# Hybrid decoder step: a head's normalising factors once instead of three times, output weights loaded one lot ahead, and high priority for bank traffic

## The chip, the cores and the metric

The kernel runs on one core of one Trainium2 chip. The metric is the device time of one execution in microseconds (us). Shown are the median and the extremes of several runs, and one more execution that the hardware profiler recorded: its span, and what each engine did in it.

## The reference

One step of a decoder layer with two parallel branches, for 1024 prompt tokens and 32 sample tokens (8 sequences of 4), model width 1024, all in float32:

```python
h, gate = adaln_in(x, c, w_ada, b_ada, g_norm)        # norm, scaled and shifted
(mq, mk, mv, mi, mf, mo, mz, aq, ak, av, az, gm, ga) = split_in(h @ w_in)
y_m, C, n, m = mlstm_branch(mq, mk, mv, mi, mf, mo, mz, C0, n0, m0, b_i, b_f, g_mn)
o = attn_prompt(q, k, v, sinks)                       # or with the cache, for the samples
y_a = o * jax.nn.silu(az)
u = jax.nn.sigmoid(gm) * (y_m @ w_mo) + jax.nn.sigmoid(ga) * (y_a @ w_ao)
x = x + gate * (u @ w_o)                              # then a last norm
...
def mlstm_chunk(carry, inp):                          # 4 heads, chunks of 128 tokens
    ...
    num = jnp.einsum('bhts,bhse->bhte', s, v) + w_inter[..., None] * jnp.einsum('bhtd,bhde->bhte', q, C)
    dot = jnp.sum(s, axis=-1) + w_inter * jnp.einsum('bhtd,bhd->bht', q, n)
    h = num / jnp.maximum(jnp.abs(dot), jnp.exp(-m_hat))[..., None]
    ...
h = h * lax.rsqrt(jnp.mean(h * h, axis=-1, keepdims=True) + NORM_EPS)
```

The division by the larger of |dot| and exp(-m_hat), followed by the root of the mean square, is what the kernel calls a head's factors.

## The kernel before

**Engines.** TensorE (PE) multiplies; ScalarE (ACT) and VectorE (DVE) move results out of its banks and form operands; SyncE (SP) issues most DMAs, ScalarE and GpSimd (POOL) a few.

**Products.** Every wide product of 1024 tokens is made of pairs: two jobs of 128 output columns together, by seven block products (numbers 1 to 7) in place of eight, on sums and differences of blocks. Each block product is 12 matmuls of 128x512, since a float32 operand is split into a high and a low part (`wh`, `wl` for weights, made by an ACT cast and a DVE subtraction) and three of the four combinations are multiplied. `pairs` lists them: four `head_in` pairs (queries, keys and values of the mLSTM heads), eight `gate` pairs (ga and gm, called ga0 to ga7 in the prediction), two `query_gate` and four `head_gate` pairs. `block_products` runs them in the order 5, 6, 2, 7, 1 of the next pair, 3, 4. A product writes to a bank: bx (products 1, 2), bw (6, 3), by (7, 4), bz (5). `filled` copies one finished bank into the next one that goes on from it, and `done` calls the kind's `evac`, which takes a finished block out (for a gate: a sum, a tanh `gt`, a store). `samples` and `samples_end` make the same jobs' sample columns (smp, smpo; a gate's `samples` takes smpo out as `gts`). `load` asks for the next pair's weights, at product 6.

**Side work.** Between a block's matmuls `side.tick()` gives other work its turn. `Side` (line 112) keeps streams of generators: m (heads, two live), a (attention units: scores sc, their transposes pt), x (sums of blocks), s (sample heads: stk, sU, sn, st, sty), g (the last modulation, then `out_weights`). A generator yields a lag and the kinds of banks that its next visit uses; the lag is counted in `side.now`, an estimate of TensorE's time. So these lags say after how much product work each visit comes. A `store` is issued by SP once 8 units have passed. PE's order is fixed by this; the order on ACT, DVE and POOL between the first part and line 2161 is not, there a scheduler picks by priority, which follows program order where nothing else is said. All banks come from four pools of two: g (bx, bw), a (by, bz), b (transposes tk, tv, ty and stk, smp, smpo, the sample heads' sU) and o (the heads' S, U, n and the sample heads' sn, st). SBUF tiles of 2 KB come from one pool (`ht`).

**A head.** `head(h)` (line 1027) goes through eight chunks in three groups of 3, 3 and 2 chunks (p = 0, 1, 2). Per group: `load` brings q, k, v, the decay matrix et and the weights qw; `prep` adds the mask; `stage_e` takes exponentials; `stage_a` transposes k and v (tk, tv) and forms S; `stage_b` makes U and, from it, the running state C of each chunk; `stage_c` makes n, copies it out as ns (into et's buffer) and sums its squares; `stage_c2` calls `factors`, a row of narrow DVE operations on 3 or 2 columns; `stage_c3` scales ns by them; `stage_d` transposes (ty) and stores. The list of visits at its end gives the order and the lags.

**Output weights.** `out_weights` (line 1924) scales the rows of w_out by the gate gb and stores what the last product needs, in six lots: four of one block row, two of two block rows from which also the sums t1 to t4 are formed. It loads a lot, waits 6 units and multiplies, one tile a visit; the sums are formed in place in the loaded tiles. `OUT_WEIGHTS = 6` starts it at product 6 of pair number 6, ga2.

Of the kernel before, what the change touches and what calls it, by code (L numbers as in the profile page):

```python
# [24 lines left out]
NS = NB * NT  # L25
# [147 lines left out]
def body(tc, a):  # L173
    nc = tc.nc
    with ExitStack() as ctx:
# [799 lines left out]
        vs = cp.tile([128, NH, NS], F32, name="vs")  # L975
        gs = cp.tile([128, NH, NS], F32, name="gs")

        def factors(dot, fl_, ssq, shape, name):
            den = sm(shape, name + "den", 2)
            V.scalar_tensor_tensor(den, dot, -1.0, dot, op0=ALU.mult, op1=ALU.max)  # L980
            V.tensor_tensor(den, den, fl_, op=ALU.max)
            V.reciprocal(den, den)
            v = sm(shape, name + "v", 2)
            V.tensor_tensor(v, den, den, op=ALU.mult)
            V.tensor_tensor(v, v, ssq, op=ALU.mult)
            V.tensor_scalar(v, v, 0.5 / 128, 0.5 * EPS, op0=ALU.mult, op1=ALU.add)
            return den, recip_sqrt(v, shape, name + "r")
# [39 lines left out]
        def head(h):  # L1027
# [71 lines left out]
            def stage_c(p):  # L1099
                cs = GROUPS[p]  # L1100
                m, j0 = len(cs), h * 8 + cs[0]
                vn, et, qw, chain, ns = w_[p]
                num = po([128, 3, 129], f"n{h}_{p}")
                for i, c in enumerate(cs):
                    mm(num[:, i], et[:, i], vn[:, i], start=True, stop=(c == 0))
                    if c:
                        mm(num[:, i], qw[:, i], chain[i], start=False, stop=True)
                S.copy(ns[:, :m], num[:, :m])
                ssq = sm([128, 3], "mssq", 2)
                for i in range(m):  # L1110
                    jk = sm([128, 128], "mjk", 2, BF16)
                    S.activation(jk, ns[:, i, 0:128], AF.Square, accum_out=ssq[:, i:i + 1])
                w_[p] = ns, ssq

            def stage_c2(p):
                m, j0 = len(GROUPS[p]), h * 8 + GROUPS[p][0]
                ns, ssq = w_[p]
                w_[p] = ns, factors(ns[:, :m, 128], fl[:, j0:j0 + m], ssq[:, :m], [128, m], f"f{m}")

            def stage_c3(p):  # L1120
                m = len(GROUPS[p])
                ns, (d, r) = w_[p]
                for i in range(m):
                    V.tensor_scalar(ns[:, i, 0:128], ns[:, i, 0:128], d[:, i:i + 1], r[:, i:i + 1], op0=ALU.mult, op1=ALU.mult)
                w_[p] = ns

            def stage_d(p):
                cs = GROUPS[p]
# [7 lines left out]
                S.activation(y, ty[:, :m].rearrange("p c e -> p (c e)"), AF.Copy, scale=gmn[:, h:h + 1])  # L1136
                issue(yhD[h][:, c0:c0 + w], y, eng=nc.gpsimd)

            for visit in ([(load, 0), 9.0, ""], [(prep, 0), 3.0, "ob"], [(stage_e, 0), (stage_a, 0), 7.0, "o"],
                          [(stage_b, 0), (load, 1), 8.0, ""], [(prep, 1), 3.0, "ob"], [(stage_e, 1), (stage_c, 0), (stage_a, 1), 3.0, ""],  # L1140
                          [(stage_c2, 0), 5.0, "o"], [(stage_b, 1), (stage_c3, 0), (load, 2), 4.0, "b"], [(stage_d, 0), 4.0, ""],
                          [(prep, 2), 3.0, "ob"], [(stage_e, 2), (stage_c, 1), (stage_a, 2), 3.0, ""], [(stage_c2, 1), 5.0, "o"],
                          [(stage_b, 2), (stage_c3, 1), 5.0, "b"], [(stage_d, 1), 5.0, "o"], [(stage_c, 2), 3.0, ""], [(stage_c2, 2), 7.0, ""],
                          [(stage_c3, 2), 5.0, "b"], [(stage_d, 2), 0.0, ""]):
                for fn, p in visit[:-2]:
                    fn(p)
                yield visit[-2:]
# [9 lines left out]
        def sample_head(h):  # L1157
# [73 lines left out]
            d, r = factors(ns[:, 128:129], fls[:, h:h + 1], ssq, [NS, 1], "fs")  # L1231
# [255 lines left out]
        def block_products(jobs, hook):  # L1487
            flat = [(0, 1)]
            for n in range(len(jobs)):
                nx = [(n + 1, 1)] if n + 1 < len(jobs) else []  # L1490
                flat += [(n, i) for i in (5, 6, 2, 7)] + nx if n else [(n, 6), (n, 2), (n, 7)] + nx + [(n, 5)]
                flat += [(n, 3), (n, 4)]

            def split_ahead(j):
                if j < len(flat):
                    jobs[flat[j][0]].split(flat[j][1])

            bank = lambda pool, name: pool([128, 512], name)
            jobs[0].load()
            yield  # L1500
            jobs[0].samples()
            split_ahead(0)
            jobs[0].first_sums()
            split_ahead(1)
            yield

            def filled(pool, name, src, n):
                b = bank(pool, name)
                if n == 0:
                    mm(b, wh[:, 0], blocks["b11"][0][0], start=True, stop=True)  # L1510
                S.copy(b, src)
                return b

            X, W, Y, Z, NX = None, None, None, None, None
            for j, (n, i) in enumerate(flat):
                job_ = jobs[n]
                nxt = jobs[n + 1] if n + 1 < len(jobs) else None
                hook(n, i)
                job_.kind.ahead(job_, i)
                if i == 6 and nxt:  # L1520
                    nxt.load()
                split_ahead(j + 2)
                if i == 1:
                    o = NX = bank(pg, "bx")
                elif i == 5:
                    o = Z = bank(pa, "bz")
                else:
                    o = {2: X, 3: W, 4: Y, 6: W, 7: Y}[i]
                new = i in (1, 5)
                wh, wl = job_.w.pop(i)  # L1530
                for k in range(4):
                    bh, bl = blocks[OPERANDS[i]][k]
                    mm(o, wh[:, k], bh, start=(new and k == 0), stop=False, more=not new)
                    mm(o, wh[:, k], bl, start=False, stop=False, more=not new)
                    mm(o, wl[:, k], bh, start=False, stop=(k == 3), more=not new)
                    if k < 3:
                        side.tick()
                if i == 6:
                    Y = filled(pa, "by", W, n)
                    job_.samples_end()  # L1540
                elif i == 2:
                    job_.done(0, 0, X)
                elif i == 5:
                    p5 = ht([128, 512], "p5")
                    S.copy(p5, Z)
                elif i == 3:
                    job_.done(0, 1, p5, W)
                elif i == 4:
                    job_.done(1, 0, Y)
                if i == (7 if n else 5):  # L1550
                    job_.done(1, 1, p5, Y)
                if i == (2 if n else 7) and nxt:
                    nxt.samples()
                    nxt.first_sums()
                if j == 0 or (i == 3 and nxt):
                    X = NX
                    W = filled(pg, "bw", X, j)
                side.tick()

        order += [("ak", 0), ("av", 0)] + [("aq", g) for g in range(4)]  # L1560
# [363 lines left out]
        def out_weights():  # L1924
# [5 lines left out]
            def keep(name, k, t):  # L1930
                woD[name, k] = dp.tile([128, 512], F32, name=f"woD{name}{k}")
                store(woD[name, k], t)

            for ks in ((4,), (5,), (6,), (7,), (0, 2), (1, 3)):
                raws = {}
                for k in ks:
                    for f in range(2):
                        raws[k, f] = ht([128, 512], f"wor{k}{f}")
                        dma(raws[k, f], a["w_out"][k * 128:(k + 1) * 128, HALF[f]])
                yield 6.0, ""  # L1940
                for (k, f), t in raws.items():
                    V.tensor_tensor(t, t, gb[f], op=ALU.mult)
                    if len(ks) == 1:
# [4 lines left out]
                if len(ks) == 2:  # L1948
                    k = ks[0]
                    b11, b12, b21, b22 = raws.values()  # L1950
                    yield 8.0, ""
                    V.tensor_tensor(b22, b22, b12, op=ALU.subtract)
                    keep("t3", k, b22)
                    yield 2.4, ""
                    V.tensor_tensor(b12, b12, b11, op=ALU.subtract)
                    keep("t1", k, b12)
                    yield 2.4, ""
                    V.tensor_tensor(b11, b11, b22, op=ALU.add)
                    keep("t2", k, b11)
                    yield 2.4, ""  # L1960
                    V.tensor_tensor(b21, b21, b11, op=ALU.subtract)
                    keep("t4", k, b21)
# [15 lines left out]
            if n == len(pairs) - 1:  # L1978
                next(att, None)

        OUT_WEIGHTS = 6
        LOADS = [(len(pairs) - 2, 7), (len(pairs) - 1, 5)]
        work = block_products(pairs, hook)
        att = att_products()
# [346 lines left out]
```

## Time and profile before

| | |
|---|---|
| Median of 3 runs | 842.65 us (842.56 to 843.61) |
| Profiled execution | 845.21 us |
| Its span | 843.4 us |
| Mean granted clock of TensorE | 0.996 |
| TensorE busy | 820.4 us (97%) |
| VectorE busy | 614.4 us (73%) |
| ScalarE busy | 422.1 us (50%) |
| GpSimd busy | 66.7 us (8%) |

The span is the recorded time from the first to the last instruction. A row of the timeline has the start in us, the length, the engine, the line of the kernel (lines 219, 246, 258 and 263 are helpers through which nearly all instructions go), the operation, the tiles it writes and reads, the shape, and in brackets how long the engine stood idle before it and whose work ended the wait. Tiles are named by the program; a matmul's length overlaps the next one's. A group row has the number of instructions with the shortest, median and longest time in ns.

### The profile page before, as it was taken

The page shows a single profiled execution, that of the slowest core. Times are in us where ns is not written, and L with a number is a line of the kernel's source. Part 1 is how long each engine was busy: PE and PEld are TensorE (multiplying, and loading weights), DVE is VectorE, ACT ScalarE, POOL GpSimd, SP SyncE. Part 2 cuts the span into 40 slices and gives each one's busy share as a digit, 9 for nine tenths or more (in the row PEclk, how much of TensorE's full clock was granted, in tenths as well). Part 3 has the DMA queues.
Part 4 walks back from the last instruction along what each step waited for, and adds up shares of the span by engine and source line. Part 5 has one row for each costly group of instructions (what it writes and reads, how often), then busy time and mean ns, then how long its engine had stood idle before and what let it go on. Part 6 is the DMA issues. An engine that isn't in the chain of part 4 may idle for free. (4 is left out here: it accounts for less than half of the span.)

```text
span 843.4 us, 15196 instructions
## 1 busy us (share of the span) xinstructions
PE 820.4 (97%) x5129; PEld 667.4 (79%) x5129; DVE 614.4 (73%) x1629; ACT 422.1 (50%) x1032; POOL 66.7 (8%) x128
## 2 busy tenths in 40 slices
PE   6999999999999999999999989999999999999996
PEld 3779897888777788888888767777777779997775
DVE  4889886656665655656586786697868998974776
ACT  5664365655465744544555534444446654334342
POOL 0120000000000000000000000001002104250000
PEclk9999999999999999999999999999999999999999
DMA  9997756356435342447866463554245685643532
GB/s 339 360 358 234 196 189 200 117 155 217 129 135 179 103 131 90 154 143 217 268 201 204 144 211 123 177 176 151 104 131 196 209 292 170 220 132 132 200 107 106
DMA packets 106690, 153.97 MB, mean 183 GB/s; under 512 B 20448, under 2 KB 54368, under 8 KB 106580
## 3 DMA queue, kind: packets, MB, share of 16 engines
q1 hardware_dynamic: 100964, 142.25, 51.8%
q10 hardware_dynamic: 4176, 6.56, 2.2%
q0 software_dynamic: 1472, 4.20, 1.3%
q8 instruction: 40, 0.66, 0.3%
q14 instruction: 38, 0.31, 0.1%
HBM read 109.22 MB, written 44.75 MB: 183 GB/s over the span
## 5 line engine op out<-in xcount | busy, mean ns | idle before, releaser
L219 ACT ACTIVATE p<-p,nmx 128x256 f32<-128x256 f32 (+1 forms) x64 | 31.0, 485 | 16.6 <-DVE nmx L219 16.3
L258 PE MATMUL g_aq<-h_h,wh_aq 128*128 128x384 f32 (+1 forms) x96 | 32.4, 338 | 0.0
L258 PE MATMUL g_w_mo<-ym_l,wh_w_mo 128*128 128x384 f32 (+1 forms) x96 | 31.1, 324 | 0.0
L258 PE MATMUL g_aq<-h_l,wh_aq 128*128 128x384 f32 (+1 forms) x96 | 31.0, 323 | 0.0
L258 PE MATMUL g_w_mo<-ym_l,wl_w_mo 128*128 128x384 f32 (+1 forms) x96 | 31.0, 323 | 0.0
L258 PE MATMUL g_aq<-h_h,wl_aq 128*128 128x384 f32 (+1 forms) x96 | 31.0, 323 | 0.0
L258 PE MATMUL g_w_mo<-ym_h,wh_w_mo 128*128 128x384 f32 (+1 forms) x96 | 31.0, 323 | 0.0
L219 DVE CUSTOM_DVE_ANT_0 p<-sc,cst,sink 128x256 f32<-128x256 f32 (+1 forms) x64 | 26.1, 463 | 4.2 <-PE sc L258 4.1
L246 POOL DMA_DIRECT2D oD<-uqv x16 | 8.9, 557 | 184.4 <-ACT uqv L219 184.4
L219 DVE COPY p<-pt 128x512 f32<-128x512 f32 (+1 forms) x16 | 10.5, 656 | 15.2 <-PE pt L263 15.2
L258 PEld LDWEIGHTS g_aq<-h_h,wh_aq 128*128 128x128 f32 x96 | 18.0, 188 | 2.6 <-issue 1.5
L219 ACT ACTIVATE et<-et,an 128x128 f32<-128x128 f32 x32 | 11.3, 395 | 15.7 <-DVE et L219 15.4
L219 ACT ACTIVATE p<-p,den 128x256 f32<-128x256 f32 (+1 forms) x32 | 14.4, 490 | 7.4 <-DVE den L219 7.3
L258 PEld LDWEIGHTS g_aq<-h_l,wh_aq 128*128 128x128 f32 x96 | 18.1, 188 | 0.0
L258 PEld LDWEIGHTS g_w_mo<-ym_h,wh_w_mo 128*128 128x128 f32 x96 | 18.0, 188 | 0.0
L258 PEld LDWEIGHTS g_w_mo<-ym_l,wh_w_mo 128*128 128x128 f32 x96 | 18.0, 188 | 0.0
L258 PE MATMUL sc<-ukv,uqv 64*128 64x256 f32 (+1 forms) x128 | 18.0, 390 | 0.0
L258 PEld LDWEIGHTS g_aq<-h_h,wl_aq 128*128 128x128 f32 x96 | 18.0, 188 | 0.0
L258 PEld LDWEIGHTS g_w_mo<-ym_l,wl_w_mo 128*128 128x128 f32 x96 | 18.0, 188 | 0.0
L263 PE MATMUL pt<-cst,p 128*128 128x128 f32 x120 | 16.5, 277 | 1.5 <-DVE mx L219 1.5
L258 PE MATMUL g_mq<-h_h,wh_mq 128*128 128x384 f32 (+1 forms) x48 | 16.8, 351 | 0.3 <-ACT mk L219 0.3
L219 ACT ACTIVATE sq<-rows_h 128x512 f32<-128x512 f32 (+2 forms) x14 | 8.1, 582 | 17.7 <-issue 12.0
(2089 smaller groups left out, 2873.6 us busy)
## 6 DMA issues: line engine op xcount, KB each, us to landing
x<-xT SPq DMA_DIRECT2D x16, 256.0 KB, 5.4
early_h<-w_ada SPq DMA_DIRECT2D x8, 512.0 KB, 9.0
adar_ga<-w_ada SPq DMA_DIRECT2D x16, 256.0 KB, 4.3
wr_ga<-w SPq DMA_DIRECT2D x16, 256.0 KB, 2.6
wr_gm<-w SPq DMA_DIRECT2D x16, 256.0 KB, 4.3
taD<-gt SPq DMA_DIRECT2D x16, 256.0 KB, 2.7
tmD<-gt SPq DMA_DIRECT2D x16, 256.0 KB, 3.2
wor<-w_out SPq DMA_DIRECT2D x16, 256.0 KB, 6.7
```

The lines of the kernel that those rows point to most:

```text
L219: ins = f(*args, **kw)
L246: ins = (eng or nc.sync).dma_start(out, in_)
L258: in_order(nc.tensor.matmul(out, lhsT, rhs, start=start, stop=stop, skip_group_check=more))
L263: in_order(nc.tensor.transpose(out, in_, idn))
```

## The change

Four things. First, `stage_c2`, once a group, becomes `stage_f`, once a head: it takes the absolute value of each group's dot (`size`) into one tile of 8 columns and calls `factors` once on all 8. All three groups' ns tiles are kept until then, and the visits of a head get other lags (9, 8 and 4 units from a load to its use become 11, 10 and 10). Second, `out_weights` starts at pair number 5 (ga1), asks for the next lot before it works on this one, and writes its sums to new tiles `wos`. Third, the next pair's weights are asked for at product 5, not 6. Fourth, `filled`, `done` and the copy of bz (`p5`) run at high priority, while `samples_end` keeps its own.

```diff
-        def factors(dot, fl_, ssq, shape, name):
-            den = sm(shape, name + "den", 2)
+        def size(den, dot):
             V.scalar_tensor_tensor(den, dot, -1.0, dot, op0=ALU.mult, op1=ALU.max)
+
+        def factors(den, fl_, ssq, shape, name):
             V.tensor_tensor(den, den, fl_, op=ALU.max)
...
                 S.copy(ns[:, :m], num[:, :m])
-                ssq = sm([128, 3], "mssq", 2)
-                for i in range(m):
+                if not p:
+                    w_["f"] = sm([128, 8], "mssq", 2)
+                ssq = w_["f"]
+                for i, c in enumerate(cs):
                     jk = sm([128, 128], "mjk", 2, BF16)
-                    S.activation(jk, ns[:, i, 0:128], AF.Square, accum_out=ssq[:, i:i + 1])
-                w_[p] = ns, ssq
-
-            def stage_c2(p):
-                m, j0 = len(GROUPS[p]), h * 8 + GROUPS[p][0]
-                ns, ssq = w_[p]
-                w_[p] = ns, factors(ns[:, :m, 128], fl[:, j0:j0 + m], ssq[:, :m], [128, m], f"f{m}")
+                    S.activation(jk, ns[:, i, 0:128], AF.Square, accum_out=ssq[:, c:c + 1])
+                w_[p] = ns
+
+            def stage_f(p):
+                den = sm([128, 8], "f8den", 2)
+                for q, cs in enumerate(GROUPS):
+                    size(den[:, cs[0]:cs[-1] + 1], w_[q][:, :len(cs), 128])
+                w_["f"] = factors(den, fl[:, h * 8:h * 8 + 8], w_["f"], [128, 8], "f8")
...
-            for visit in ([(load, 0), 9.0, ""], [(prep, 0), 3.0, "ob"], [(stage_e, 0), (stage_a, 0), 7.0, "o"],
-                          [(stage_b, 0), (load, 1), 8.0, ""], [(prep, 1), 3.0, "ob"], [(stage_e, 1), (stage_c, 0), (stage_a, 1), 3.0, ""],
-                          [(stage_c2, 0), 5.0, "o"], [(stage_b, 1), (stage_c3, 0), (load, 2), 4.0, "b"], [(stage_d, 0), 4.0, ""],
-                          [(prep, 2), 3.0, "ob"], [(stage_e, 2), (stage_c, 1), (stage_a, 2), 3.0, ""], [(stage_c2, 1), 5.0, "o"],
-                          [(stage_b, 2), (stage_c3, 1), 5.0, "b"], [(stage_d, 1), 5.0, "o"], [(stage_c, 2), 3.0, ""], [(stage_c2, 2), 7.0, ""],
-                          [(stage_c3, 2), 5.0, "b"], [(stage_d, 2), 0.0, ""]):
+            for visit in ([(load, 0), 11.0, ""], [(prep, 0), 3.0, "ob"], [(stage_e, 0), (stage_a, 0), 7.0, "o"],
+                          [(stage_b, 0), (load, 1), 10.0, ""], [(prep, 1), 3.0, "ob"],
+                          [(stage_e, 1), (stage_c, 0), (stage_a, 1), 7.0, "o"],
+                          [(stage_b, 1), (load, 2), 10.0, ""], [(prep, 2), 3.0, "ob"],
+                          [(stage_e, 2), (stage_c, 1), (stage_a, 2), 7.0, "o"], [(stage_b, 2), 5.0, "o"],
+                          [(stage_c, 2), 5.0, ""], [(stage_f, 0), 4.0, ""], [(stage_c3, 0), 4.0, "b"],
+                          [(stage_d, 0), (stage_c3, 1), 4.0, "b"], [(stage_d, 1), (stage_c3, 2), 4.0, "b"], [(stage_d, 2), 0.0, ""]):
...
-                if i == 6 and nxt:
+                if i == (5 if n else 6) and nxt:
                     nxt.load()
...
+                with tc.high_priority():
+                    if i == 6:
+                        Y = filled(pa, "by", W, n)
+                    elif i == 2:
+                        job_.done(0, 0, X)
+                    elif i == 5:
+                        p5 = ht([128, 512], "p5")
+                        S.copy(p5, Z)
+                    elif i == 3:
+                        job_.done(0, 1, p5, W)
+                    elif i == 4:
+                        job_.done(1, 0, Y)
+                    if i == (7 if n else 5):
+                        job_.done(1, 1, p5, Y)
                 if i == 6:
-                    Y = filled(pa, "by", W, n)
                     job_.samples_end()
...
                     X = NX
-                    W = filled(pg, "bw", X, j)
+                    with tc.high_priority():
+                        W = filled(pg, "bw", X, j)
...
-            for ks in ((4,), (5,), (6,), (7,), (0, 2), (1, 3)):
+            def load(ks):
                 raws = {}
                 for k in ks:
                     for f in range(2):
                         raws[k, f] = ht([128, 512], f"wor{k}{f}")
                         dma(raws[k, f], a["w_out"][k * 128:(k + 1) * 128, HALF[f]])
-                yield 6.0, ""
+                return raws
+
+            def summed(n, k, x, y, op):
+                t = ht([128, 512], f"wos{n}{k}")
+                V.tensor_tensor(t, x, y, op=op)
+                keep(n, k, t)
+                return t
+
+            lots = (4,), (5,), (6,), (7,), (0, 2), (1, 3)
+            ahead = [load(lots[0])]
+            yield 5.0, ""
+            for i, ks in enumerate(lots):
+                raws = ahead.pop()
+                if i + 1 < len(lots):
+                    ahead.append(load(lots[i + 1]))
+                yield 3.0, ""
                 for (k, f), t in raws.items():
                     V.tensor_tensor(t, t, gb[f], op=ALU.mult)
...
-                    yield 8.0, ""
-                    V.tensor_tensor(b22, b22, b12, op=ALU.subtract)
-                    keep("t3", k, b22)
+                    t3 = summed("t3", k, b22, b12, ALU.subtract)
                     yield 2.4, ""
...
-        OUT_WEIGHTS = 6
+        OUT_WEIGHTS = 5
```

The sums t1, t2 and t4 are changed as t3 is, and the sample heads call `size` and `factors` one after the other.

More of the change, by code (lines that the diff above doesn't have):

```diff
@@ L1108, in stage_c @@
                 S.copy(ns[:, :m], num[:, :m])
-                ssq = sm([128, 3], "mssq", 2)
-                for i in range(m):
+                if not p:
+                    w_["f"] = sm([128, 8], "mssq", 2)
+                ssq = w_["f"]
+                for i, c in enumerate(cs):
                     jk = sm([128, 128], "mjk", 2, BF16)
-                    S.activation(jk, ns[:, i, 0:128], AF.Square, accum_out=ssq[:, i:i + 1])
-                w_[p] = ns, ssq
-            def stage_c2(p):
-                m, j0 = len(GROUPS[p]), h * 8 + GROUPS[p][0]
-                ns, ssq = w_[p]
-                w_[p] = ns, factors(ns[:, :m, 128], fl[:, j0:j0 + m], ssq[:, :m], [128, m], f"f{m}")
-            def stage_c3(p):
[L1121 to L1125, printed above, removed]
+                    S.activation(jk, ns[:, i, 0:128], AF.Square, accum_out=ssq[:, c:c + 1])
[5 more added lines that the diff above has]
+                w_["f"] = factors(den, fl[:, h * 8:h * 8 + 8], w_["f"], [128, 8], "f8")
+            def stage_c3(p):
+                ns, (d, r) = w_[p], w_["f"]
+                for i, c in enumerate(GROUPS[p]):
+                    V.tensor_scalar(ns[:, i, 0:128], ns[:, i, 0:128], d[:, c:c + 1], r[:, c:c + 1], op0=ALU.mult, op1=ALU.mult)
             def stage_d(p):
@@ L1230, in sample_head @@
             yield 2.5, ""
-            d, r = factors(ns[:, 128:129], fls[:, h:h + 1], ssq, [NS, 1], "fs")
+            den = sm([NS, 1], "fsden", 2)
+            size(den, ns[:, 128:129])
+            d, r = factors(den, fls[:, h:h + 1], ssq, [NS, 1], "fs")
             yield 4.0, ""
@@ L1537, in block_products @@
                         side.tick()
+                with tc.high_priority():
[12 more added lines that the diff above has]
+                        job_.done(1, 1, p5, Y)
                 if i == 6:
-                    Y = filled(pa, "by", W, n)
                     job_.samples_end()
[L1541 to L1551, printed above, removed]
                 if i == (2 if n else 7) and nxt:
@@ L1950, in out_weights @@
                     b11, b12, b21, b22 = raws.values()
-                    yield 8.0, ""
-                    V.tensor_tensor(b22, b22, b12, op=ALU.subtract)
-                    keep("t3", k, b22)
+                    t3 = summed("t3", k, b22, b12, ALU.subtract)
                     yield 2.4, ""
-                    V.tensor_tensor(b12, b12, b11, op=ALU.subtract)
-                    keep("t1", k, b12)
+                    summed("t1", k, b12, b11, ALU.subtract)
                     yield 2.4, ""
-                    V.tensor_tensor(b11, b11, b22, op=ALU.add)
-                    keep("t2", k, b11)
+                    t2 = summed("t2", k, b11, t3, ALU.add)
                     yield 2.4, ""
-                    V.tensor_tensor(b21, b21, b11, op=ALU.subtract)
-                    keep("t4", k, b21)
+                    summed("t4", k, b21, t2, ALU.subtract)
                     yield 2.4, ""
```

## The prediction

> **What bounds the kernel now.** I read the page's head first, then the waits of TensorE, then the timeline around each wait.
>
> ```profile
> span 843.4 us, 15196 instructions
> PE 820.4 (97%) x5129; PEld 667.4 (79%) x5129; DVE 614.4 (73%) x1629; ACT 422.1 (50%) x1032; POOL 66.7 (8%) x128
> ```
>
> TensorE (PE) is busy for 820.4 of 843.4 us, so the time can only fall where PE stands still or runs slowly. The change leaves PE's 4241 instructions of the compiled program as they are and moves them about; VectorE's (DVE) fall from 1616 to 1488, ScalarE's stay at 943. So the question is which stalls of PE go and which come. The waits of PE say what the first kind is (columns: who waits and for whom, us in all, times, longest):
>
> ```profile
> PE smpo L258 <- DVE Cs L219: 2.3, 1, 2.3
> PE pt L263 <- DVE mx L219: 1.5, 2, 1.0
> PE tv L263 <- ACT gts L219: 1.3, 2, 0.7
> PE bw L258 <- ACT bw L219: 0.9, 1, 0.9
> ```
>
> The other waits (6.4 us at the start, 0.7 and less elsewhere) lie in the first 200 us or after 640 us, where the instructions of both programs stand in the same order. The four rows lie between 200 and 500 us, where the order changes.
>
> **The largest one, step by step.** The timeline of PE, then of DVE, then the window that holds them (start, length, instruction, and in brackets the idle time before it and who ended it; the window's row has PE, PEld, DVE, ACT, POOL, then the granted clock):
>
> ```profile
> 485.32 0.39 PE L258 MATMUL bw<-t2l,wh_pgate__5788 128*128 128x512 f32 x1
> 485.55 0.39 PE L258 MATMUL bw<-t2h,wl_pgate__5789 128*128 128x512 f32 x1
> 488.28 0.69 PE L258 MATMUL smpo<-cst,smps 128*128 128x64 f32 x2 [2.34 <-DVE Cs L219]
> 491.43 0.38 PE L258 MATMUL sU<-vm,skn 96*128 96x258 f32 x1
> 484.10 0.69 DVE L219 TENSOR_TENSOR wor<-wor,gb 128x512 f32<-128x512 f32 x1 [2.88 <-DMA wor<-w_out]
> 485.26 0.69 DVE L219 TENSOR_TENSOR wor<-wor,gb 128x512 f32<-128x512 f32 x1 [0.47 <-DMA wor<-w_out]
> 486.48 1.28 DVE L219 TENSOR_TENSOR wor<-wor,gb 128x512 f32<-128x512 f32 x2
> 487.68 1.01 DVE L219 TENSOR_TENSOR Cs<-Cs,sU 128x387 f32<-128x387 f32 x2
> 450.00:500.00 50.00, 47.66 (x292) 37.83 (x291) 36.80 (x111) 24.26 (x61) 3.59 (x14) 0.97 0.57 187
> ```
>
> The sample head's product smpo needs a bank that sU holds until DVE has added it to Cs. DVE stood 2.88 and 0.47 us on loads of output weights, then worked off three more multiplications, and only then came Cs. A wide product follows another after 0.23 us (485.32 to 485.55), so smpo was due at 485.78 and came at 488.28: 2.50 us lost. Then two smpo and six wide products took 3.15 us to 491.43. The same work at full pace is 0.17 for the pair (357.50 to 357.67 below) and 6 x 0.23, together 1.55. So the slow clock after the gap cost 1.60 us, and the place 4.1 us.
>
> **The smaller ones.** Each gap also loses the 0.16 us by which a product of 0.39 overlaps the next at a spacing of 0.23. The two pt gaps cost 1.5 + 0.32 = 1.8 us, the two tv gaps 1.3 + 0.32 = 1.6. Of bw's 0.9 I count only 0.2: its copy follows a product that ends just before, and high priority can remove only the cast ahead of it. Sum: 4.1 + 1.8 + 1.6 + 0.2 = 7.7 us.
>
> **Factors once per head.** Before pt, DVE is late with the softmax's maximum because it has worked off a chain of narrow operations on 128x3 tiles:
>
> ```profile
> L219 DVE TENSOR_TENSOR f3r_w<-f3r_w,f3v x24: 151/161/165, 242.0 to 467.2; 128x3 f32<-128x3 f32 x24
> 245.40 0.69 DVE L219 TENSOR_TENSOR wl_phead_in__3190<-wr_mv,wh_phead_in__3189 128x512 fp32r<-128x512 f32 x1 [0.48 <-ACT wh_phead_in__3189 L219]
> 246.01 0.48 DVE L219 CUSTOM_DVE_ANT_0 p<-sc,cst,sink 128x256 f32<-128x256 f32 x1
> ```
>
> 12 chains of 17 become 4 of 19: 204 - 76 = 128 operations x 0.161 = 20.6 us of DVE, all beside PE, worth only the stall it feeds. In the new order pt of that unit stands ahead of its scores' successor, and the other unit's pt has nine products after its scores with no chain on DVE between: both gaps go (1.8 us). At the new f8 chain (19 x 0.161 = 3.1 us at the head's end) only the head's own ty is due from DVE, and that two visits of four lag units later; I cost it at nothing, and at 0.5 us at most if a score unit falls there.
>
> **High priority.** Both tv gaps have one pattern:
>
> ```profile
> 357.50 0.33 PE L258 MATMUL smpo<-cst,smps 128*128 128x64 f32 x2
> 357.67 0.50 PE L263 MATMUL tk<-cst,hk 128*128 128x128 f32 x3
> 357.51 0.62 ACT L219 CAST wh_pgate__4449<-wr_ga 128x512 fp32r<-128x512 f32 x1 [1.69 <-issue]
> 358.04 0.58 ACT L219 COPY by<-bw 128x512 f32<-128x512 f32 x1
> 358.56 0.21 ACT L219 ACTIVATE gts<-smpo 128x64 f32<-128x64 f32 x1
> ```
>
> smpo and tv share the b banks, and gts, which empties smpo, stands behind a cast and a copy. In the new order tk and tv no longer follow smpo directly, so the 1.6 us go by the order, not by the priority. But the priority puts the copy `by<-bw`, which has to wait for bw's last product, ahead of what else ScalarE (ACT) could do. At pair ga0 smpo now comes three products after S1_2, and needs the bank that the copy of tv1_2 frees; ACT has et's copy and three squares first. 0.48 for the copy of 387 columns and three squares at 0.2 to 0.3 against 9 + 3 products: I take 0.4 us, bounds 0 and 0.7.
>
> **Output weights.** They start one product earlier in the list (about 26 us), load a lot ahead and keep sums in new tiles. What the loads cost now, and how long they take (last column: us from issue to landing):
>
> ```profile
> DVE wor L219 <- DMA wor<-w_out: 7.4, 5, 2.9
> DVE et L219 <- DMA et<-nmd: 8.1, 5, 2.3
> wor<-w_out SPq DMA_DIRECT2D x16, 256.0 KB, 6.7
> taD<-gt SPq DMA_DIRECT2D x16, 256.0 KB, 2.7
> et<-nmd SPq DMA_DIRECT2D x8, 192.0 KB, 4.0
> ```
>
> A load that is issued one lot of 7.8 lag units ahead has its 6.7 us, so the 7.4 us of DVE waits go, and the sample head's burst no longer meets them: the 4.1 us are saved. But loading ahead, new tiles and three live groups fill the pool of 2 KB tiles: by the first and last use of each in the compiled programs, 43 of 48 places are taken at head 3's loads, 35 before. There et's load takes the buffer of a tanh tile gt, so SyncE (SP) holds it until the store taD<-gt has landed, and behind it stand qw's load and the next stores; on DVE the next weights' split and sums stand behind et's addition. With t the end of bx of pair ga3's product 2:
>
> ```profile
> L219 ACT ACTIVATE gt<-bx x8: 582/591/611, 337.3 to 516.7; 128x512 f32<-128x512 f32 x8
> L219 DVE TENSOR_TENSOR et<-et,cst x12: 415/550/559, 188.8 to 449.6; 128x384 f32<-128x384 f32 x8, 128x256 f32<-128x256 f32 x4
> L219 DVE SCALAR_TENSOR_TENSOR C<-C,dec,U x28: 341/346/352, 214.5 to 475.4; 128x129 f32<-128x129 f32 x28
> 492.82 0.40 PE L258 MATMUL bx<-h_h,wl_pgate__5817 128*128 128x512 f32 x1
> 494.16 0.50 PE L258 MATMUL by<-t3h,wh_pgate__5866 128*128 128x512 f32 x1
> ```
>
> gt is ready at t + 0.8 (0.59 and a start), its store's issue and 2.7 us end at t + 3.8 (0.3 more for the queue), et's load lands 4.0 to 5.8 us later (the later end is an estimate: the median plus most of the 2.3 us by which DVE waited at worst): t + 7.8 to t + 9.6. DVE's addition (0.55) and then the third C of head 3 (0.35) stand in order behind it: t + 8.7 to t + 10.5. This C frees the bank for S2_2 of head 2. PE reaches S2_2 after the sixteen narrow smp (1.34 by the last two rows), 18 wide products (4.14) and 13 small ones at about 0.12 (1.6) and some switches: t + 7.4. So PE stalls 1.3 to 3.1 us; I take 2.0, near the 4.0 us landing plus a little. Below nothing is excluded, as nothing here starts earlier. At the long end the clock falls as at 488: the bounds are 0 (a buffer that lands earlier) and 3.1 + 1.6.
>
> The row at 488 shows a gap of 2.34 us followed by 0.43 us a product instead of 0.23. [...]
>
> **Sample head 2.** Its stk2 now stands in the middle of query-gate pair 1's product 2. DVE then runs its burst between the load of bx and its use zt:
>
> ```profile
> 592.71 0.28 DVE L219 TENSOR_TENSOR skn<-stk,skn 32x128 fp32r<-32x128 f32 x1
> 596.96 0.29 DVE L219 CAST vm<-vf 32x258 fp32r<-32x258 f32 x1
> L219 DVE SCALAR_TENSOR_TENSOR zt<-zt,bx x2: 679/679/679, 539.7 to 561.6; 128x512 f32<-128x512 f32 x2
> ```
>
> The burst took 4.54 us (592.71 to 597.25). In the new order it has a weight split and two sums (0.7 each) in it as that one has; with skn's 0.4 us of start, some 0.7 for what stands between and zt's 0.68 it ends about 6.3 us after stk2. PE's cover is sS2 and 6 wide products (1.5), smp (1.2) and 12 wide (2.8): 5.4 to 5.5. Then bx of head-gate pair 0 waits for zt's bank: 0.9, and with the restart 0.16 and one more operation at most 1.6. I take 1.2; the lower bound is 0, if the casts of vm run ahead on ACT.
>
> **Next weight load at product 5.** One product earlier on SP (2.8 us); no trace row shows PE waiting for these loads, so nothing is gained; in the queue it may stand ahead of head loads, which is in the bounds above.
>
> **Sum.** Saved 7.7, new 2.0 + 1.2 + 0.4 = 3.6, net -4.1 us. The profiled execution took 845.21 us (1.8 around the span), so it would take 841.1; it lies 2.56 above the median 842.65, where the same difference gives 838.6. The ends: new stalls 0 to 4.7 + 1.6 + 0.7 = 7.0 and 0.5 for f8.
>
> **Rivals.** (a) No new stall: loads land early and ACT and DVE keep up, 842.65 - 7.7 = 835.0. For it speaks that DVE loses 20.6 us of work; against it the pool's 43 of 48. Chance 0.20. (b) The output weights still hold DVE where a sample product waits: SP serves loads in order, behind stores that wait for sums. Then the 4.1 us stay and, with the 3.6, nothing is left: 842.7. Against it, the lots end about 54 us earlier, before the burst. Chance 0.10. (c) The slow clock at 488 comes not from the gap but at a time of its own: 1.6 stay, 840.2. Chance 0.07. [...] (d) The other side: the full pool. A second head load (hq, hk or et of head 3's third group) waits for a store as et does. Each such gap over about 2.3 us costs 4.1 as at 485; two of them with 1.6 from the other places are 9.8, so 842.65 - 7.7 + 9.8 = 844.8. It decides from 9.4 us of new loss on. For it: DVE already waits five times for et. Against it: only one such place shows in the order. Chance 0.17.
>
> **Numbers.** The forecast keeps 0.46, with its own range 836.0 to 842.0 (new stalls 1.0 to 7.0). About 0.2% (1.7 us) is what a measurement can tell from none. Faster by more: forecast, (a) and (c), 0.73, less 0.03 for the forecast's upper end: 0.70. Same: (b) and that end, 0.13. Slower: 0.17. The range 834.8 to 843.0 leaves out (d) and little else.
>
> **What would show it.** In the profile after: no row smpo <- Cs, pt <- mx, tv <- gts between 200 and 600 us; DVE's wait for wor near 0 and its busy time about 594; a row S <- DVE C of 1 to 3 us near ga4, a row bx <- DVE zt near 1 at head-gate 0; the clock back to 1.00 in the stage around 485. A wait of DVE for et over 4 us, or a second gap with clock below 1.00, would prove (d). If S and bx don't wait, (a) is right; if wor stays, (b).

## The result

The changed kernel is slower, not faster: median 846.26 us of five runs (845.89 to 849.29) against 842.92 (842.56 to 845.38) of the kernel before; ratio 1.0043 (95% interval 1.0029 to 1.0056). A second comparison on another chip gave 1.0052 (1.0036 to 1.0069), and its profile shows the largest wait below again, with 3.1 us. The profiled execution took 845.89 us, the shortest of the five.

The head of the page after, and the stages around 400 and 485 us (columns as before), then 400 to 450 us of the kernel before:

```profile
span 844.1 us, 15042 instructions
PE 821.2 (97%) x5129; PEld 668.2 (79%) x5129; DVE 598.8 (71%) x1501; ACT 421.4 (50%) x1032; POOL 66.4 (8%) x128
400.00:450.00 50.00, 46.03 (x289) 38.04 (x287) 31.07 (x74) 23.66 (x65) 0.31 (x3) 0.97 0.59 193
450.00:500.00 50.00, 50.00 (x312) 40.38 (x311) 36.13 (x91) 25.74 (x61) 4.32 (x14) 1.00 0.46 148
```

```profile
400.00:450.00 50.00, 49.33 (x314) 41.16 (x313) 37.27 (x109) 26.49 (x71) 1.46 (x5) 1.00 0.75 239
```

VectorE has 15.6 us less to do, where 20.6 were forecast, and TensorE's stage around 485 runs without a gap, as forecast. But between 400 and 450 us TensorE now stands still for 4.0 us, where it stood 0.7, and its granted clock there is 0.97. The waits of TensorE after:

```profile
PE S L258 <- DVE C L219: 4.0, 1, 4.0
PE sc L258 <- DVE p L219: 0.9, 1, 0.9
PE bx L258 <- DVE zt L219: 0.8, 1, 0.8
PE bw L258 <- ACT bw L219: 0.7, 1, 0.7
PE smpo L258 <- ACT hv L219: 0.3, 1, 0.3
PE sc L258 <- DVE C L219: 0.2, 1, 0.2
```

All rows that were to go are gone (smpo <- Cs, both pt <- mx, both tv <- gts), and the three places that were to come have come. One of them is twice its size, and sc <- p was not foreseen. VectorE's own waits name the common cause:

```profile
DVE et L219 <- DMA et<-nmd: 18.0, 7, 5.0
DVE wor L219 <- DMA wor<-w_out: 8.4, 3, 6.4
```

It stands 18.0 us on the heads' decay matrices et where it stood 8.1. Its waits for the output weights, which were to go, are still there, 8.4 us where they were 7.4; the longest, 6.4 us, ends at 387.65, and TensorE does not wait there. The timeline at the largest wait, TensorE, VectorE, ScalarE and SyncE's queue in turn:

```profile
409.55 0.40 PE L258 MATMUL bx<-h_h,wl_pgate__4806 128*128 128x512 f32 x1
417.35 0.38 PE L263 MATMUL tv<-cst,hv 128*128 128x128 f32 x2
421.69 0.71 PE L258 MATMUL S<-hq,hk 128*128 128x128 f32 x4 [3.96 <-DVE C L219]
422.16 0.47 PE L258 MATMUL bx<-h_h,wh_pgate__4880 128*128 128x512 f32 x1
423.42 0.63 PE L258 MATMUL bx<-h_l,wh_pgate__4880 128*128 128x512 f32 x1
426.35 0.39 PE L258 MATMUL bw<-h_h,wl_pgate__4947 128*128 128x512 f32 x1
413.54 0.35 DVE L219 SCALAR_TENSOR_TENSOR C<-C,dec,U 128x129 f32<-128x129 f32 x1
415.10 0.69 DVE L219 TENSOR_TENSOR wl_pgate__5024<-ws,wh_pgate__5023 128x512 fp32r<-128x512 f32 x1 [1.21 <-ACT wh_pgate__5023 L219]
420.82 0.56 DVE L219 TENSOR_TENSOR et<-et,cst 128x384 f32<-128x384 f32 x1 [5.03 <-DMA et<-nmd]
421.29 0.34 DVE L219 SCALAR_TENSOR_TENSOR C<-C,dec,U 128x129 f32<-128x129 f32 x1
411.14 0.61 ACT L219 ACTIVATE gt<-bx 128x512 f32<-128x512 f32 x1
412.73 0.38 SPq L246 DMA_DIRECT2D taD<-gt  x1
414.60 0.45 SPq L246 DMA_DIRECT2D hv<-vD  x1
416.24 0.32 SPq L246 DMA_DIRECT2D et<-nmd  x1
```

The third C of head 3 needs nothing that comes so late: its second C was made at 413.54, and where the order on VectorE is another (below), the third is made at 417.06. It is late because the mask's addition to et stands ahead of it in VectorE's order, and that addition waits for a load. The load was issued at 416.24, once the store of gt, issued at 412.73, had landed and given up the buffer (SyncE's queue stood 1.1 us on that store), and needed 4.6 us more. S was due at 417.57 (two tv from 417.35 on, 0.11 apart) and came at 421.69: 4.1 us. Then eleven spacings from 422.16 to 426.35 took 4.19 us in place of 11 x 0.23 = 2.53: 1.7 us more for the clock.

### The profile page after: what moved, and what is told of

The parts are those of the page before. It is cut to its first block, busy times and chain, and to the rows that moved or that the text cites. A ratio compares the mean times of both kernels' runs of the same rounds, so it can differ in the third digit from the quotient of the medians.

```text
span 844.1 us, 15042 instructions
## 1 busy us (share of the span) xinstructions
PE 821.2 (97%) x5129; PEld 668.2 (79%) x5129; DVE 598.8 (71%) x1501; ACT 421.4 (50%) x1032; POOL 66.4 (8%) x128
## 4 chain that ended last, share of the span: by engine, by line
PE 91%; DMA 3%; DVE 3%; issue 1%; ACT 1%; SPq 0%; DVEq 0%; ACTq 0%
PE bw L258 11%; PE bx L258 11%; PE by L258 11%; PE bz L258 6%; PE g_aq L258 6%; PE g_w_mo L258 6%; PE g_mq L258 3%; PE foW L258 3%; PE foX L258 3%; PE foY L258 2%; PE smp L258 2%; PE sc L258 2%; PE oT L258 2%; PE foZ L258 2%; PE pt L263 2%; PE n L258 2%
## 5 line engine op out<-in xcount | busy, mean ns | idle before, releaser
L219 DVE TENSOR_TENSOR et<-et,cst 128x384 f32<-128x384 f32 (+1 forms) x12 | 6.1, 511 | 18.0 <-DMA et<-nmd 18.0
```

The source lines that it names most:

```text
L219: ins = f(*args, **kw)
```

## The experiments

Each ratio is to the kernel before, run beside it on the same chip. The chips differ (before took from 843.0 to 845.3 us in the median), so kernels are compared by their ratios.

**The kernel before, profiled again.** No edit.

> The kernel before, unchanged, profiled once more. The change's median is 3.3 us above that of before, though the two profiled spans differ by 0.7 us only. Theory C: the profiled execution of before was a slow one, 2.56 us above its median, because its loads of output weights landed late and made the stall at 485 us (4.1 us with the clock) longer than usual; then this profile shows smpo <- Cs well under 2.3 us, no slow clock there, and about 842.7 us. Rival: the stall at 485 is always there and the 2.56 us lie elsewhere (start, end, or around the span); then the gap of 2.3 us and the slow products are there again.

Ratio 0.9993 (0.9977 to 1.0009), 845.49 us in the profile, with this wait:

```profile
PE smpo L258 <- DVE Cs L219: 2.2, 1, 2.2
```

Theory C did not come true: the long stall and the slow products were there again. But this execution, too, took 845.49 us, longer than the 842.92 that the change was compared with. The next two, with the same order on TensorE as before, say more.

**High priority alone, and the weights' load at product 5 alone.**

```diff
+                with tc.high_priority():      # kernel prio_only: only these lines of the change
...
-                if i == 6 and nxt:            # kernel load5_only: only this one
+                if i == (5 if n else 6) and nxt:
```

> Of the change the high priority alone. I expect nothing to measure: the tv <- gts waits (0.7 each) stay, as the cast and copy keep their place; ratio 0.999 to 1.001. Rival: the priority puts copies that wait for a product's end ahead of others' on ScalarE, and a new wait of 0.5 to 1 us comes: 1.001 to 1.002.

> Of the change the weights' load at product 5 alone. I expect nothing to measure: 0.999 to 1.001. Rival: on SyncE the load stands ahead of a head's loads and makes them late: a wait S <- C or U <- hk of 0.5 us or more, ratio above 1.001.

0.9998 (0.9988 to 1.0008) and 1.0006 (0.9994 to 1.0018): neither can be told from nothing. The profiled execution of the first took 842.10 us, near the first median of before. Its row of the waits and TensorE's timeline at that place:

```profile
PE smpo L258 <- DVE Cs L219: 1.3, 1, 1.3
484.99 0.39 PE L258 MATMUL bw<-t2h,wl_pgate__5789 128*128 128x512 f32 x1
486.63 0.43 PE L258 MATMUL smpo<-cst,smps 128*128 128x64 f32 x2 [1.26 <-DVE Cs L219]
487.19 0.39 PE L258 MATMUL bx<-h_l,wh_pgate__5816 128*128 128x512 f32 x1
487.42 0.40 PE L258 MATMUL bx<-h_h,wl_pgate__5817 128*128 128x512 f32 x1
```

Here the same stall costs 1.41 us (486.63 against 485.22 due), and the products after it keep 0.23 us. The way to the next sU (488.35) takes 1.72 us in place of the 1.55 of the prediction, so the place costs 1.6 us in all. The profile of load5_only, 845.73 us, has 2.3 us again with slow products. So the execution from which the prediction took its largest saving was one of the long ones: 4.1 us there, 1.6 in one of 842 us. The mean granted clock of the executions without a profile fits this. On the chip of prio_only all 17 of before had 0.997 to 0.999, while the four profiles with slow products at this place (before, before_again, load5_only, before_room) had 0.993 to 0.996. On the chip of before_again, where before took 845.3 us in the median, 15 of its 29 executions had 0.996 or less; that each of these had the long stall is not shown.

**The heads' part alone, and the output weights' part alone.**

```diff
# head_only: factors, stage_f, the visits and lags     # ow_only: load ahead, wos, OUT_WEIGHTS = 5
```

> Of the change the part of the heads alone: factors once, other lags; output weights, priority and weight loads as before. My steps: pt <- mx (1.8 us) and tv <- gts (1.6) go, bx <- zt (0.9), smpo <- hv (0.4) and sc near 289 (1.2) come; the output weights are late again beside the sample heads (as at 485 us of before, 0 to 4 us). S waits for C behind et, but the buffer comes free earlier: 0 to 1.5 us. Sum 0 to -3 against 842.9 where the 485 stall is small: 841.5, bounds 839.5 to 844. Rival: the head's new lags alone bring the whole S stall: 846 or more.

> Of the change the output weights alone: begun at ga1, loaded a lot ahead, sums in new tiles. My step: the wait smpo <- Cs (2.2 to 2.3 us) and the slow products after it go, 3 to 4 us of 845 where before shows them, since all lots end before the sample heads' products: ratio 0.995 to 0.998. Rival: three more operations on loads stand on VectorE beside the heads between 380 and 440 us, and waits of the heads' products take their place: ratio 1.000 or more.

0.9991 (0.9975 to 1.0006) and 1.0052 (1.0040 to 1.0064). The heads' part trades its waits: pt and tv are gone, sU <- Cs 1.8, sc <- p 0.8, S <- C 0.6 and bx <- zt 0.8 are there. TensorE's order is that of the changed kernel, and S waits 0.6 us where it waits 4.0 there. The output weights' part loses on its own what the whole change loses. Its waits of TensorE and VectorE's timeline:

```profile
PE tv L263 <- ACT gts L219: 2.7, 2, 2.1
PE bw L258 <- DVE wor L219: 1.9, 1, 1.9
373.12 0.69 DVE L219 TENSOR_TENSOR wl_pgate__4561<-wr_ga,wh_pgate__4560 128x512 fp32r<-128x512 f32 x1
377.45 0.56 DVE L219 TENSOR_TENSOR et<-et,cst 128x384 f32<-128x384 f32 x1 [3.64 <-DMA et<-nmd]
379.19 0.69 DVE L219 TENSOR_TENSOR wor<-wor,gb 128x512 f32<-128x512 f32 x1
379.80 0.68 DVE L219 TENSOR_TENSOR gt<-p,bw 128x512 f32<-128x512 f32 x1
381.05 0.58 ACT L219 COPY bw<-bx 128x512 f32<-128x512 f32 x1
381.68 0.78 PE L258 MATMUL bw<-t2h,wh_pgate__4560 128*128 128x512 f32 x1 [1.90 <-DVE wor L219]
```

(The last two rows are ScalarE's and TensorE's.) The row names wor, but that operation only ended last; what held VectorE are the head's loads before: 3.64 us on et and 0.62 on qw, then wor, then the gt that reads bw, and only then can ScalarE's copy fill bw's bank, whose end at 381.63 lets TensorE go on. The smpo <- Cs row is gone, as the step said; a larger one has come.

**The order on VectorE.** The changed kernel, with the mask's addition put behind the C operations that come before it in the program:

```diff
-                V.tensor_tensor(et[:, :m], et[:, :m], cmask.unsqueeze(1).to_broadcast((128, m, 128)), op=ALU.add)
+                ins = V.tensor_tensor(et[:, :m], et[:, :m], cmask.unsqueeze(1).to_broadcast((128, m, 128)), op=ALU.add)
+                no_sync(getattr(ins, "ins", ins), [last[n] for n in ("C",) if n in last])
...
+                last["C"] = getattr(ins, "ins", ins)      # in stage_b, after its last C
```

> The changed kernel, with one order added on VectorE: a head's addition of the mask to et (which waits for a load) comes after the state sums C that stand ahead of it in the program. Same loads, same buffers, same order on PE. Theory A: the 3.96 us wait of S for C, with the slow products after it (4.1 + 1.6), and the two waits of sc near 289 us (1.2) are nothing but C and the copies standing behind this addition; then both go and the time falls from 846.3 by 6 to 7 to 839.5 (838.8 to 841). Rival B: ScalarE stands on the same et for 6.4 us, with the copy of n behind it, and PE meets that wait a little later: above 843.5.

> The changed kernel with the order C before et again, beside the two others on one chip: it was 0.9952 of before on a chip on which before took 845.3 us. If that gain was partly the slower executions of before there, it is now nearer to 1: the waits that go are 5 to 7 us of the changed kernel's 846.5, so 840 to 841.5 against 843 of before: 0.997 to 0.998. Rival: again 0.9952 or less.

0.9952 (0.9932 to 0.9971) and, on the second chip, 0.9968 (0.9955 to 0.9981), between what theory and rival said of the repetition. TensorE's order and every load are those of the changed kernel. VectorE's timeline in the first of the two:

```profile
417.06 0.35 DVE L219 SCALAR_TENSOR_TENSOR C<-C,dec,U 128x129 f32<-128x129 f32 x1 [0.65 <-PE n L258]
421.97 0.56 DVE L219 TENSOR_TENSOR et<-et,cst 128x384 f32<-128x384 f32 x1 [4.56 <-DMA et<-nmd]
```

VectorE still stands 4.56 us on the load, but C is made at 417.06 and no S <- C row is left. In the first profile 1.3 us of it came back as by <- gt, since a gate's sum stood behind the addition too; in the second that wait is absent, but sc waits 0.7 us for a C near 289 us, which the theory had put at nothing.

**The operation on another engine.** The changed kernel, its two preparing operations on GpSimd:

```diff
-                V.tensor_tensor(et[:, :m], et[:, :m], cmask.unsqueeze(1).to_broadcast((128, m, 128)), op=ALU.add)
-                V.tensor_tensor(qw[:, :m], qw[:, :m], q[:, :m * 128].rearrange("p (c e) -> p c e", e=128), op=ALU.mult)
+                G.tensor_tensor(et[:, :m], et[:, :m], cmask.unsqueeze(1).to_broadcast((128, m, 128)), op=ALU.add)
+                G.tensor_tensor(qw[:, :m], qw[:, :m], q[:, :m * 128].rearrange("p (c e) -> p c e", e=128), op=ALU.mult)
```

> The changed kernel with a head's two preparing operations (mask added to et, qw times q) on GpSimd, PE's order the same. Theory A: VectorE then never stands on a head's load: S <- C and sc <- p go, as with the order C before et (0.9952 of before there), and the by <- gt wait of 1.3 us that was left there too, if GpSimd needs no more than 2 us for the addition: ratio to before 0.992 to 0.996. Rival: GpSimd's slower additions make et late for ScalarE, whose exponentials hold back its copies, and PE meets that: ratio 0.998 or more.

1.0076 (1.0063 to 1.0088): the rival, and worse than it said. The waits of TensorE, and then ScalarE's timeline:

```profile
PE tv L263 <- ACT smps L219: 6.3, 1, 6.3
393.06 0.40 ACT L219 ACTIVATE et<-et,an 128x128 f32<-128x128 f32 x1 [7.42 <-POOL et L219]
393.37 0.24 ACT L219 COPY smps<-smp 128x128 f32<-128x128 f32 x1
```

ScalarE waits in its own order for the same et (7.42 us), and behind the exponential stands the copy that empties a bank. The addition itself takes 0.86 us on GpSimd by the profile (0.55 on VectorE), 0.3 more; that is little beside a wait of 7.42, so it isn't what decides.

**The buffer.** First with the output weights started at ga2 again, then with one place more in the pool of 2 KB tiles:

```diff
-        OUT_WEIGHTS = 5
+        OUT_WEIGHTS = 6                                   # after_ow6
...
-                self.sums = ht([128, 128], "smps")
+                self.sums = sm([128, 128], "smps", 1)     # after_room: no longer a tile of the pool
```

> The changed kernel with the output weights started at ga2 as before (OUT_WEIGHTS = 6). Theory A2 (buffers): at head 3's second load et then takes a buffer whose store was issued some 10 us earlier, so its load is issued 2 to 2.7 us sooner and the wait of S falls from 4.0 to 1.0 to 2.0 us without slow clock: 842 to 843.5. Rival: the load is late because of the queue itself (other transfers in flight), then S waits 3.5 us or more again and the time stays within 1 us of 846.3.

> The changed kernel with one tile (the samples' sums, smps, 0.5 KB) taken out of the pool of 2 KB tiles, so that the pool has one more place; PE's order the same. By the places of the tiles, et at head 3's second load then no longer follows gt, whose store had to land first (2.7 to 3.5 us), but a tile that PE has read shortly before. Theory A2: its load is issued 2 to 3 us sooner, the wait S <- C falls from 3.1 to 4.0 us to 0.5 to 1.5 without slow clock, and the ratio from 1.0052 to 1.000 to 1.002. Rival: other queued transfers make the load late, S waits 3 us or more, ratio 1.004 or more.

after_ow6: 1.0010 (0.9992 to 1.0027). SyncE issued et's load at 412.74, 3.5 us earlier, and S waited 2.9 us in place of 4.0: the addition was done sooner, but a wait of 1.37 us for qw's load had come between it and C. So the wait lay between what the theory (1.0 to 2.0) and the rival (3.5 or more) said. This profile is of the shortest of twelve executions (843.22 to 849.07 us), so it says little of the median.

after_room: 0.9960 (0.9947 to 0.9973), 3.5 us below before where the change had been 3 to 4 above. TensorE's order is unchanged. SyncE's queue, VectorE's timeline and TensorE's wait:

```profile
412.98 0.39 SPq L246 DMA_DIRECT2D et<-nmd  x1
413.48 0.36 SPq L246 DMA_DIRECT2D taD<-gt  x1
417.47 0.56 DVE L219 TENSOR_TENSOR et<-et,cst 128x384 f32<-128x384 f32 x1 [2.09 <-DMA et<-nmd]
PE S L258 <- DVE C L219: 1.0, 1, 1.0
```

The load of et now goes out before the store of gt, not after its landing. It is 3.3 us earlier, lands as fast (4.5 us), and S waits 1.0 us without slow products after it. The sc wait near 289 us, which the theory did not count, is gone as well; a wait of tv for p of 1.0 us near 264 has come. The ratio is lower than the theory's 1.000 to 1.002, and how much of that is the sc wait is not shown.

**Both.**

> The changed kernel with both: C before et on VectorE, and one place more in the pool. If the two act on the same wait, the second adds only what was left with the order alone (by <- gt 1.3, U <- hk 0.7): up to 2 us less than with the order alone, ratio to before 0.993 to 0.996 (it was 0.9952). Rival: those two waits do not come from et's load, and the ratio is that of the order alone.

0.9947 (0.9935 to 0.9959), 838.96 us against 843.73 of before on that chip. This version beats both kernels: no wait S <- C, sc <- p, by <- gt or U <- hk is left.

**Is it the place alone?** The same line of edit on the kernel before, on the output weights' part and on the heads' part:

> The kernel before with the samples' sums smps taken out of the pool of 2 KB tiles, so that it has one place more. If the lack of places is the change's own (43 of 48 taken at head 3's loads against 35 before), before gains nothing: ratio 0.998 to 1.001, with smpo <- Cs, pt <- mx and tv <- gts still there. Rival: the place alone is worth the 4 us that it brought the changed kernel, in both: ratio 0.995 to 0.997.

> The output weights' part alone with one place more. If its loss (1.0052, with bw <- wor 1.9 us, slow products after it, and tv <- gts 2.1) comes from loads that wait for places, both waits fall under 1 us and the ratio is 0.997 to 1.000. Rival: VectorE stands on the weights themselves, which are asked for too late behind other stores whatever the places: the two waits stay, ratio 1.003 or more.

> The heads' part alone with one place more: it was 0.9991, with sU <- Cs 1.8 us and slow products after it from the late output weights, sc <- p 0.8 and S <- C 0.6. The last two may go (1.5 us), the first stays: ratio 0.996 to 0.999. Rival: nothing changes, 0.999 or more.

0.9992 (0.9978 to 1.0005), 1.0035 (1.0019 to 1.0051) and 0.9998 (0.9981 to 1.0016). The kernel before gains nothing from the place, so the gain of after_room belongs to the change. Neither part gains alone; for both the rival came. In head_room sc <- p is gone, but S <- C is 1.4 us, where it was 0.6 and was to go, and tv <- p 1.2 has come. In ow_room the wait only moved:

```profile
PE bw L258 <- DVE et L219: 2.1, 1, 2.1
PE tv L263 <- ACT gts L219: 2.1, 2, 1.4
```

So the output weights begun earlier gain only with the heads' part (whether by its lags or by its single call of factors is not separated); the heads' part alone still meets output weights beside the sample heads (sU <- Cs 2.0 in head_room); and both together need the place or the order.

## Why the prediction was wrong

It forecast -4.1 us; +3.3 came. Three steps make the difference.

**The largest saving was read from one long execution.** The step "the place 4.1 us" is right for that profile, and the prediction noted that the profile lay 2.56 us above the median. It then took the full saving off the median ("the same difference gives 838.6"). In an execution of 842.10 us with the same order the place costs 1.6 us. So the savings were 7.7 - 2.5 = 5.2.

**S <- C was sized at 2.0 and measured 4.1, and 1.7 for the clock.** The mechanism is the one described, and one place more in the pool takes the wait from 4.0 us to 1.0. The step that failed is the chain of times from t, the end of pair ga3's product 2, at 409.9. Its terms were too short in the queues: gt was ready at t + 1.8, not 0.8, for ScalarE had stood 2.32 us on VectorE's output weights until 409.00 and had two copies, two casts and gts first; its store was issued at t + 2.8, not at 1.1; et's load at t + 6.3, not at 3.8. So et was there at t + 10.9, beyond the later end, 9.6. Of the 3.1 us by which it came after the earlier end, 7.8, the way to the store's issue made 1.7 and the two transfers 1.4 (3.5 from the store to the load where 2.7 was put, 4.6 for the load where 4.0 was). The 4.7 us of the upper end were not enough for the 5.8 that came. The count of 43 of 48 places stands in no run, and the kernel's pool has 50 (`bufs=50`, line 194); that the load waited for this store is what SyncE's queue shows.

**A second place of the same kind was missed.** The step "both gaps go (1.8 us)" is right, but head 1's et, for which VectorE stood 4.32 us, holds the copy of p, and with it sc, near 289 us:

```profile
287.20 0.56 DVE L219 TENSOR_TENSOR et<-et,cst 128x384 f32<-128x384 f32 x1 [4.32 <-DMA et<-nmd]
288.91 0.68 DVE L219 COPY p<-pt 128x512 f32<-128x512 f32 x1
```

From the last product before sc (288.40) to the first behind it (291.56) TensorE takes 3.16 us; in after_room, where sc doesn't wait, it takes 1.38 (289.77 to 291.15). So this place costs 1.8 us. The prediction asked for each place whether an operation stands behind a load, but only where a buffer looked late. Its rival (d), at 0.17, came nearest: two gaps of this kind, 844.8 us, with a wait of VectorE for et over 4 us as its sign, which came twice (5.03 and 4.32). But its second gap was to be a load that waits for a store in head 3's third group. Head 1's et waited for no store: it was issued at 282.04, behind a load of gate weights (wr_gm) for which SyncE had stood 2.9 us on VectorE.

**The small ones were right.** bx <- zt was forecast at 1.2 and cost 0.92 (0.8 and the overlap), smpo at ga0 0.4 and cost 0.44; factors once ended both pt waits, though VectorE's busy time fell by 15.6 us and not by 20.6; the tv waits went with the order; priority and the earlier load are worth nothing that can be measured.

The sum with measured terms: -5.2 + 4.1 + 1.7 + 1.8 + 0.9 + 0.4 = +3.7. The medians differ by 3.3, and the two profiled executions from which most terms are read, of prio_only and of the changed kernel, by 3.8. Each term comes from single executions, so closer than some tenths the sum can't be.

The step that VectorE's 7.4 us on output weights go was wrong too (8.4 are left), but what rival (b) made of it, a sample product that waits for them, did not happen in the changed kernel. Rival (a), all 7.7 us saved, was out of reach: with order and place together the gain is 4.8 us (838.96 against 843.73).

What stays open: the change was not tried with loads asked for still earlier, so it is not shown whether more lead alone would have done what the place did. Nor is it shown why a place more is enough when, by the prediction's count, places were free.

## What to carry to other kernels

Here an operation that waited for a load held what stood behind it on its engine: VectorE's 5.03 us on et held a C of 0.34 us until 421.29, and put ahead of et, in after_c_before_et, this C came at 417.06. Before a load is moved, doubled or given less room, look at what stands behind its first use, and put nothing there that frees a bank. When more tiles are kept alive in a shared pool, ask of each load whose buffer it takes: the load that followed a store's landing paid both transfers (3.5 and 4.6 us here), and one place more turned the sign of the change (1.0043 and 1.0052 without it, 0.9960 with it). And a saving read from one profile is first set against the spread of the executions: the stall of smpo, which hangs on loads, was 2.34 us in before and 1.26 in prio_only, with the same order on TensorE.

## What was not expected of the hardware

In these profiles the slow clock did not go by the length of the gap. Products came 0.43 us apart in place of 0.23 after gaps of 1.78 us (head_only), 1.90 (ow_only), 2.00 (before_room), 2.20 (before_again), 2.34 (before) and 3.96 (changed kernel), and did not after 1.26 (prio_only), 1.98 (head_room), 2.09 (a second gap of ow_only) and 2.95 (after_ow6). They began at once in before (488.28) and 1.3 us after the gap's end in the changed kernel (421.69 to 422.99). The stretches lasted 3.2 us (before, 488.28 to 491.43) and 3.4 (changed kernel, 422.99 to 426.35), but 6.1 in load5_only (487.41 to 493.47, after a gap of 2.33). The mean granted clock of that execution of load5_only was 0.993, where the profiled one of before had 0.996.

Rival (c) of the prediction, a slow clock at a time of its own, is not borne out: in no profile here does such a stretch of wide products between 180 and 660 us come without a gap of 1.78 us or more before it. But a gap of that length was followed by one in some executions and not in others, and what decides is not shown.
